# Transposing 8192 x 8192 in fp32: two PSUM counters merged into one, and the load's wait moved onto the first transpose

## The chip, the cores and the metric

One core of a Trainium2 chip. The metric is the device time of one execution in microseconds (us), median of several runs. A difference of under 2% counts as "same".

In the lines of the profile, PE stands for TensorE's matmuls (a transpose is one of them), PEld for its weight loads, DVE for VectorE, ACT for ScalarE; a q behind the name is the engine's sequencer, which waits, branches and issues. `in` is a load buffer, `ps` PSUM, `regs` a store region. L118 is line 118 of that run's kernel, and the numbers shift from kernel to kernel. A semaphore is used in this program as a counter that one side raises (`then_inc`, `sem_inc`) and an engine waits for (`wait_ge`, `wait_op`). A load is said to have landed when its semaphore has the last of the 16 increments that the load's wait asks for.

## The reference

```python
def setup_inputs():
    return {"x": np.random.randn(8192, 8192).astype(np.float32)}

def reference(x):
    return np.transpose(x)
```

268.44 MB have to be read from HBM and 268.44 MB written to it.

## The kernel before

The input is taken in 128 steps. Each step is a chunk of 128 rows x 4096 columns (2 MB), loaded into one of three SBUF buffers. TensorE transposes it in 32 pieces of 128 x 128 into PSUM: 16 pieces fill the first half (`pss[0]`), 16 the second (`pss[1]`). ScalarE copies the first half out into a ring of store regions, VectorE the second half. ScalarE also issues all stores and all loads but the first three, in program order.

TensorE's program is a loop; it waits for the load, then for each half of PSUM:

```python
def transposes(k):
    nc.tensor.sem_inc(s_ld[k], -16).wait_op(s_ld[k], 16, "sem-ge")        # L112
    for q in range(NR):                                                   # NR = 8
        e, g = divmod(q, NH)                                              # NH = 4
        if g == 0:
            nc.tensor.sem_inc(s_bank[e], -1).wait_op(s_bank[e], 1, "sem-ge")   # L116
        for b in range(B):                                                # B = 4
            tr = nc.tensor.transpose(pss[e][...], ins[k][...], ident)     # L118
        if q % 2:
            tr.then_inc(s_pe, 1)
...
for e in range(2):
    nc.tensor.sem_inc(s_bank[e], 1)          # both halves free at the start
nc.tensor.wait_ge(s_id, 2)                   # identity built by GpSimd
```

The copies wait for `s_pe`, and the last of a half gives that half back:

```python
for t, (s, c) in enumerate(chunks):
    for e in range(2):
        eng = (nc.scalar, nc.vector)[e]
        ...                                   # wait for a region's store where a new one begins
        for u in runs:                        # 1 to 4 copies a half
            eng.wait_ge(s_pe, t * NH + (e * NH + u[-1]) // 2 + 1)
            cp = nc.scalar.copy(out=o, in_=i) if e == 0 else nc.vector.tensor_copy(out=o, in_=i)   # L216
            ...
            if u is runs[-1]:
                ...
                cp.then_inc(s_bank[e], 1)     # this half of PSUM is free
            for q in ends:
                store(q, e, copied[e])        # issued by ScalarE
    if t + NIN < T:                           # NIN = 3
        nc.scalar.wait_ge(s_pe, (t + 1) * NR // 2)
        load(t + NIN)                         # into the buffer just transposed
```

Of the kernel before, what the change touches and what calls it, by code (L numbers as in the profile page):

```python
# [39 lines left out]
@with_exitstack  # L40
def kernel(
    ctx: ExitStack,
    tc: tile.TileContext,
    x: bass.AP,
    out: bass.AP,
):








    nc = tc.nc
    P = 128
    N, M = x.shape
    assert x.shape == out.shape[::-1]
    dt = x.dtype

    S = 32
    B = 4
    W = 8
    NR = S // B
    NIN = 3
    NREG = 9
    CH = N // P
    J = S * P

    with tc.tile_critical():  # L70
        nc.alloc_sbuf_tensor("pad", [P, 32], dt)
        ident = nc.alloc_sbuf_tensor("ident", [P, P], dt).ap()
        ins = [nc.alloc_sbuf_tensor(f"in{k}", [P, J], dt).ap() for k in range(NIN)]
        SIZE = B * W * P
        regs = nc.alloc_sbuf_tensor("regs", [P, NREG * SIZE], dt).ap()
        NH = NR // 2
        pss = [nc.alloc_psum_tensor(f"ps{k}", [P, NH * B * P], dt).ap() for k in range(2)]

        s_id = nc.alloc_semaphore("s_id")
        s_ld = [nc.alloc_semaphore(f"s_ld{k}") for k in range(NIN)]  # L80
        s_st = [nc.alloc_semaphore(f"s_st{k}") for k in range(NREG)]
        s_bank = [nc.alloc_semaphore("s_banka"), nc.alloc_semaphore("s_bankv")]
        s_pe = nc.alloc_semaphore("s_pe")
        s_cp = [nc.alloc_semaphore("s_cpa"), nc.alloc_semaphore("s_cpv")]

        nc.gpsimd.memset(ident, 0.0).then_inc(s_id, 1)  # L86
        nc.gpsimd.wait_ge(s_id, 1)
        nc.gpsimd.affine_select(  # L88
            out=ident,
            in_=ident,  # L90
            compare_op=mybir.AluOpType.not_equal,
            fill=1.0,
            base=0,
            pattern=[[-1, P]],
            channel_multiplier=1,
        ).then_inc(s_id, 1)

        chunks = [(s, c) for s in range(M // J) for c in range(CH)]

        def load(t):  # L100
            s, c = chunks[t]
            (nc.sync if t < NIN else nc.scalar).dma_start(
                out=ins[t % NIN], in_=x[c * P:(c + 1) * P, s * J:(s + 1) * J]
            ).then_inc(s_ld[t % NIN], 16)






        def transposes(k):
            nc.tensor.sem_inc(s_ld[k], -16).wait_op(s_ld[k], 16, "sem-ge")  # L112
            for q in range(NR):
                e, g = divmod(q, NH)
                if g == 0:
                    nc.tensor.sem_inc(s_bank[e], -1).wait_op(s_bank[e], 1, "sem-ge")  # L116
                for b in range(B):
                    tr = nc.tensor.transpose(  # L118
                        pss[e][:, (g * B + b) * P:(g * B + b + 1) * P],
                        ins[k][:, q * B * P + b:(q + 1) * B * P - B + b + 1:B],  # L120
                        ident,
                    )
                if q % 2:
                    tr.then_inc(s_pe, 1)



        T = len(chunks)
        assert T % NIN == NIN - 1
        pe = [nc.tensor.engine]  # L130
        for e in range(2):
            nc.tensor.sem_inc(s_bank[e], 1)
        nc.tensor.wait_ge(s_id, 2)
        with nc.Fori(0, T // NIN + 1, engines=pe) as turn:
            with nc.tensor.If(turn > 0):
                transposes(NIN - 1)
            for k in range(NIN - 1):
                transposes(k)

        for t in range(NIN):  # L140
            load(t)

        copied = [0, 0]
        free = list(range(NREG))
        stored = [0] * NREG
        window = {}

        def store(q, e, count):
            t0, r, parts = window.pop(q)
            nc.scalar.wait_ge(s_cp[e], count)  # L150
            base = 0
            for s, a, z in parts:
                rows = (z - a) * P
                j0 = s * J + q * B * P
                dst = out[j0:j0 + B * P, a * P:a * P + rows]
                dst = dst.rearrange("(q b) i -> q b i", q=P)
                src = regs[:, r * SIZE + base:r * SIZE + base + B * rows]
                base += B * rows
                if any(stored):
                    st = wide_dma(nc, nc.scalar, "qActDynamicHW", dst, src)  # L160
                else:
                    st = nc.scalar.dma_start(
                        out=dst, in_=src.rearrange("q (b i) -> q b i", b=B)
                    )
                st.then_inc(s_st[r], 16)
                stored[r] += 1
            free.append(r)

        def closes(w, t):
            t0, r, parts = w  # L170
            return t + 1 == t0 + sum(z - a for _, a, z in parts)
# [5 lines that stand above are left out]
                place = []  # L177
                for q in range(e * NH, (e + 1) * NH):
                    if q not in window:



                        span = (q - c) % W + 1
                        r = free.pop(0)
                        parts = [(s, c, min(c + span, CH))]
                        if c + span > CH and t + span < T:
                            parts.append((s + 1, 0, c + span - CH))
                        window[q] = (t, r, parts)
                        if stored[r]:
                            eng.wait_ge(s_st[r], 16 * stored[r])  # L190
                    t0, r, parts = window[q]
                    k = [p[0] for p in parts].index(s)
                    base = r * SIZE + B * P * sum(z - a for _, a, z in parts[:k])
                    _, a, z = parts[k]
                    place.append((base + (c - a) * P, (z - a) * P))

                runs = []
                for g in range(NH):
                    if runs:
                        u = runs[-1]  # L200
                        gap = place[g][0] - place[g - 1][0]
                        if place[g][1] == place[u[0]][1] and abs(gap) < 2 ** 15 and (
                            len(u) == 1 or gap == place[u[1]][0] - place[u[0]][0]
                        ):
                            u.append(g)
                            continue
                    runs.append([g])
                for u in runs:
                    off, dist = place[u[0]]
                    gap = place[u[-1]][0] - place[u[-2]][0] if len(u) > 1 else 0  # L210
                    dims = [list(regs.ap[0]), [gap, len(u)], [dist, B], [1, P]]
                    o = bass.AP(regs.tensor, regs.offset + off, dims)
                    i = pss[e][:, u[0] * B * P:(u[-1] + 1) * B * P]
                    i = i.rearrange("p (l b i) -> p l b i", b=B, i=P)
                    eng.wait_ge(s_pe, t * NH + (e * NH + u[-1]) // 2 + 1)  # L215
                    cp = nc.scalar.copy(out=o, in_=i) if e == 0 else nc.vector.tensor_copy(out=o, in_=i)  # L216
                    ends = [e * NH + g for g in u if closes(window[e * NH + g], t)]
                    if ends:
                        cp.then_inc(s_cp[e], 1)
                        copied[e] += 1  # L220
                    if u is runs[-1]:
                        if ends:
                            eng.wait_ge(s_cp[e], copied[e])
                            eng.sem_inc(s_bank[e], 1)
                        else:
                            cp.then_inc(s_bank[e], 1)
                    for q in ends:
                        store(q, e, copied[e])
            if t + NIN < T:
                nc.scalar.wait_ge(s_pe, (t + 1) * NR // 2)  # L230
                load(t + NIN)
        for r in range(NREG):
            nc.sync.wait_ge(s_st[r], 16 * stored[r])
# [30 lines left out]
```

## Time and profile before

| | before |
|---|---|
| time, median of 3 runs | 1264.1 us (1263.37 to 1264.13) |
| span of the profiled run | 1262.4 us |
| TensorE busy | 749.6 us, 59% |
| VectorE, ScalarE busy | 24%, 20% |
| DMA | 425 GB/s over the span |
| landing of one load to the next | 9.76 us (median) |

How to read it: here no compute engine is busy over 59%, the DMA digits are 9 in 39 of 40 slices, and the GB/s row lies between 413 and 431 from the second slice to the 39th.

### The profile page before, as it was taken

To read this page: it belongs to the slowest core of one execution; us is meant where nothing else is said; L and a number is where in the kernel's file an instruction comes from. 1 tells how busy PE (TensorE), PEld (TensorE's weight loads), DVE (VectorE), ACT (ScalarE), POOL (GpSimd) and SP (SyncE) were. 2 spreads that over 40 slices of the span, in tenths; PEclk is the share of its full clock that TensorE was granted. 3 is DMA by queue.
4 is the path that set the end of the run, shared out by engine and by line. 5 is a ranking of instruction groups with operands and counts; after the bars stand their busy time and mean duration, and the time that the engine had idled before them with its cause. 6 is when DMAs were issued, how large, how long until landed. Compare 5 with 4: busy or idle time off the path is not lost. (4 is left out here: it accounts for less than half of the span.)

```text
span 1262.4 us, 9794 instructions
## 1 busy us (share of the span) xinstructions
PE 749.6 (59%) x4096; PEld 729.1 (58%) x4096; DVE 302.7 (24%) x250; ACT 252.8 (20%) x257; POOL 0.7 (0%) x6
## 2 busy tenths in 40 slices
PE   6566555656566555656566655666565655666561
PEld 6565555655566555655565655656565655666561
DVE  2322222222222222222222222222222222222220
ACT  3212121121111211122211121121112211121120
POOL 0000000000000000000000000000000000000000
PEclk9967777686767777686866787777768687776865
DMA  9999999999999999999999999999999999999998
GB/s 381 429 429 428 430 430 428 430 429 431 428 430 430 429 428 431 429 429 430 429 423 413 431 428 431 428 430 429 431 428 430 429 430 430 429 430 429 430 419 346
DMA packets 39273, 536.97 MB, mean 425 GB/s; under 512 B 4320, under 2 KB 4832, under 8 KB 6240
## 3 DMA queue, kind: packets, MB, share of 16 engines
q10 hardware_dynamic: 38832, 530.60, 98.8%
q1 hardware_dynamic: 432, 6.29, 1.2%
q14 instruction: 8, 0.07, 0.0%
q8 instruction: 1, 0.02, 0.0%
HBM read 268.44 MB, written 268.44 MB: 425 GB/s over the span
## 5 line engine op out<-in xcount | busy, mean ns | idle before, releaser
L118 PE MATMUL ps<-ident,in 128*128 128x128 f32 x4096 | 749.6, 366 | 486.2 <-PEq L116 486.1
L118 PEld LDWEIGHTS ps<-ident,in 128*128 128x128 f32 x4096 | 729.1, 220 | 506.5 <-issue 506.5
L216 DVE COPY regs<-ps 128x512 f32<-128x512 f32 (+3 forms) x250 | 302.7, 1246 | 934.4 <-PE ps L118 823.4
L216 ACT COPY regs<-ps 128x512 f32<-128x512 f32 (+3 forms) x256 | 251.5, 1015 | 981.9 <-PE ps L118 491.1
L216 ACT ACT_TABLE_LOAD x1 | 1.3, 1283 | 0.9 <-SPq L70 0.9
L88 POOL TENSOR_SCALAR_AFFINE_SELECT ident<-ident 128x128 f32<-128x128 f32 x1 | 0.3, 294 | 0.2 <-POOL ident L86 0.2
L86 POOL MEMSET ident<- 128x128 f32 x1 | 0.2, 205 | 0.5 <-SPq L70 0.5
L248 POOL MEMSET const-bfloat16-1.0<- 128x1 bf16 x1 | 0.1, 102 | 0.0
L248 POOL MEMSET const-uint8-127<- 128x1 uint8 x1 | 0.1, 102 | 0.0
L248 POOL MEMSET const-float32-0.0<- 128x1 f32 x1 | 0.1, 99 | 0.2 <-issue 0.2
L248 POOL MEMSET const-float32-1.0<- 128x1 f32 x1 | 0.1, 99 | 0.0
## 6 DMA issues: line engine op xcount, KB each, us to landing
in<-in_x_dram ACTq DMA_DIRECT2D x125, 2048.0 KB, 21.7
out_dram<-regs ACTq DMA_DIRECT2D x114, 2048.0 KB, 17.5
out_dram<-regs ACTq DMA_DIRECT2D x4, 1792.0 KB, 17.4
in<-in_x_dram SPq DMA_DIRECT2D x3, 2048.0 KB, 11.7
out_dram<-regs ACTq DMA_DIRECT2D x4, 1536.0 KB, 14.8
out_dram<-regs ACTq DMA_DIRECT2D x4, 1280.0 KB, 15.2
out_dram<-regs ACTq DMA_DIRECT2D x4, 1024.0 KB, 15.5
out_dram<-regs ACTq DMA_DIRECT2D x4, 768.0 KB, 16.4
```

The source lines that it names most:

```text
L86: nc.gpsimd.memset(ident, 0.0).then_inc(s_id, 1)
L88: nc.gpsimd.affine_select(out=ident, in_=ident, compare_op=mybir.AluOpType.not_equal, fill=1.0, base=0, pattern=[[-1, P]], channel_multipl ...
L118: tr = nc.tensor.transpose(pss[e][:, (g * B + b) * P:(g * B + b + 1) * P], ins[k][:, q * B * P + b:(q + 1) * B * P - B + b + 1:B], ident,)
L216: cp = nc.scalar.copy(out=o, in_=i) if e == 0 else nc.vector.tensor_copy(out=o, in_=i)
L248: nc = _bacc.Bacc("TRN2", target_bir_lowering=False, num_devices=1)
```

## The change

The intent is to have fewer instructions on TensorE's sequencer: one wait for PSUM a step, not two; the load's wait carried by the first transpose; and no start-up increments, since GpSimd sets PSUM free when the identity is built. As written, TensorE has nine semaphore instructions fewer: two in each of the three steps of its loop's body, and three before the loop.

```diff
-        s_bank = [nc.alloc_semaphore("s_banka"), nc.alloc_semaphore("s_bankv")]
+        s_bank = nc.alloc_semaphore("s_bank")
...
         nc.gpsimd.affine_select(...)
-        ).then_inc(s_id, 1)
+        ).then_inc(s_bank, 2)
...
         def transposes(k):
-            nc.tensor.sem_inc(s_ld[k], -16).wait_op(s_ld[k], 16, "sem-ge")
+            nc.tensor.sem_inc(s_bank, -2).wait_op(s_bank, 2, "sem-ge")
             for q in range(NR):
                 e, g = divmod(q, NH)
-                if g == 0:
-                    nc.tensor.sem_inc(s_bank[e], -1).wait_op(s_bank[e], 1, "sem-ge")
                 for b in range(B):
                     tr = nc.tensor.transpose(...)
+                    if q == b == 0:
+                        tr.wait_op(s_ld[k], 16, "sem-ge").then_inc(s_ld[k], -16)
...
-        for e in range(2):
-            nc.tensor.sem_inc(s_bank[e], 1)
-        nc.tensor.wait_ge(s_id, 2)
...
-                            cp.then_inc(s_bank[e], 1)
+                            cp.then_inc(s_bank, 1)
```

There is a second effect beside the count. With one counter that must reach 2, TensorE cannot start the first half of a step before VectorE has copied the second half of the step ahead.

More of the change, by code (lines that the diff above doesn't have):

```diff
@@ L223 @@
                             eng.wait_ge(s_cp[e], copied[e])
-                            eng.sem_inc(s_bank[e], 1)
+                            eng.sem_inc(s_bank, 1)
                         else:
-                            cp.then_inc(s_bank[e], 1)
+                            cp.then_inc(s_bank, 1)
                     for q in ends:
```

## The prediction

> **What bounds the kernel now.** I read the page first (busy shares, slices, DMA queues), then the waits, then the timeline at the start, in the middle and at the end, then the same stretches as a table of windows.
>
> The page:
>
> ```profile
> PE 749.6 (59%) x4096; PEld 729.1 (58%) x4096; DVE 302.7 (24%) x250; ACT 252.8 (20%) x257; POOL 0.7 (0%) x6
> DMA  9999999999999999999999999999999999999998
> GB/s 381 429 429 428 430 430 428 430 429 431 428 430 430 429 428 431 429 429 430 429 423 413 431 428 431 428 430 429 431 428 430 429 430 430 429 430 429 430 419 346
> q10 hardware_dynamic: 38832, 530.60, 98.8%
> in<-in_x_dram ACTq DMA_DIRECT2D x125, 2048.0 KB, 21.7
> ```
>
> No engine is busy over 59% of the span, while the DMA engines are at nine tenths or more in every slice but the last, and move 428 to 431 GB/s from the second slice to nearly the end. The bytes are fixed: 268.44 MB in, 268.44 MB out. 536.9 MB at 429 GB/s is 1251.5 us; the span is 1262.4. So at most 11 us of the whole program are anything but transfers at the rate that they show. The last line gives the depth of the queue: a load lands 21.7 us after its issue, and a step (one 128x4096 chunk) takes 9.76 us (median distance of two loads' landings), so about two steps of work stand in the queue all the time.
>
> Where is the DMA not full? The windows (length; busy us of PE, PEld, DVE, ACT, POOL; clock; DMA share; GB/s):
>
> ```profile
> 0.00:2.00 2.00, 0.00 (x0) 0.00 (x0) 0.00 (x0) 1.10 (x1) 0.70 (x6) 1.00 0.19 41
> 2.00:1227.00 1225.00, 742.94 (x4064) 722.60 (x4064) 299.91 (x246) 249.32 (x253) 0.00 (x0) 0.75 1.01 428
> 1227.00:1229.00 2.00, 0.00 (x0) 0.00 (x0) 0.31 (x1) 0.00 (x0) 0.00 (x0) 0.83 0.64 270
> 1229.00:1256.00 27.00, 6.65 (x32) 6.49 (x32) 2.50 (x4) 2.35 (x4) 0.00 (x0) 0.56 1.00 419
> 1256.00:1263.00 7.00, 0.00 (x0) 0.00 (x0) 0.00 (x0) 0.00 (x0) 0.00 (x0) 0.50 0.13 56
> ```
>
> For 1225 us the share is 1.01. Idle are the first 2 us, some 0.7 us at 1227 to 1229, and the run-out after 1256.
>
> The waits say what TensorE waits for:
>
> ```profile
> PE ps L118 <- PEq L116: 486.1, 126, 8.6
> ACT regs L216 <- DMA out_dram<-regs: 478.8, 61, 10.2
> ```
>
> The 486 us look like a wait for PSUM (L116), the very wait that the change merges. That is a trap: L116 is only the last of the sequencer's instructions before the matmul. In the trace's records the wait for the load (L112) starts 0.03 us after the load's sixteenth completion, the first L116 some 0.15 us later, and the first weight load 0.26 us after the landing, in nearly every step. So TensorE waits for data.
>
> [...] two L116 instructions stand 0.17 us apart although each shows 0.05 us. [...] Here all stores and all loads but three are issued by ScalarE in program order, which the change does not touch: only a gap in the queue could change the time, not an order.
>
> **The change, part by part.**
>
> 1. One counter in place of two. Before, TensorE may write the first half of PSUM as soon as ScalarE has copied it, and the second half as soon as VectorE has. Now a step starts when both have copied. What counts is the room between the last copy's end of step t and the landing of load t+1. The steady state looks like this (start, length, engine):
>
> ```profile
> 1042.97 5.56 PE L118 MATMUL ps<-ident,in 128*128 128x128 f32 x32 [4.19 <-PEq L116]
> 1047.65 1.87 ACT L216 COPY regs<-ps 128x2048 f32<-128x2048 f32 x1 [7.84 <-DMA out_dram<-regs]
> 1048.57 2.29 DVE L216 COPY regs<-ps 128x2048 f32<-128x2048 f32 x1 [7.46 <-PE ps L118]
> 1052.74 6.16 PE L118 MATMUL ps<-ident,in 128*128 128x128 f32 x32 [4.21 <-PEq L116]
> ```
>
> The last copy ends at 1048.57 + 2.29 = 1050.86, TensorE starts again at 1052.74 because the load landed at 1052.45: 1.6 us of room. I listed this for all 127 step changes from the trace's records. From step 5 on the room is never negative: median 1.59 us, least 0.38 us (after step 55). Put the other way, matmuls 5.6 us (6.7 at worst, under a lowered clock) plus 1.9 us (2.6 at worst) until the last copy's end make 7.5 us, 9.4 at worst, in a step of 9.76 us. So the merged wait should cost TensorE nothing there.
>
> At the start it does bind. The three first loads land at 8.28, 13.10 and 18.13, closer than a step:
>
> ```profile
> 8.56 14.10 PE L118 MATMUL ps<-ident,in 128*128 128x128 f32 x96 [8.56 <-PEq L116]
> 13.67 2.48 DVE L216 COPY regs<-ps 128x512 f32<-128x512 f32 x4 [13.67 <-PE ps L118]
> 17.54 2.48 DVE L216 COPY regs<-ps 128x512 f32<-128x512 f32 x4 [1.39 <-PE ps L118]
> 21.73 2.48 DVE L216 COPY regs<-ps 128x512 f32<-128x512 f32 x4 [1.71 <-PE ps L118]
> ```
>
> VectorE's copies of step 0 end at 16.15, but step 1 began at 14.31. It will now begin at about 16.2 and end its matmuls at about 20.3 (4.1 us at full clock). VectorE ends 1.55 us after that, at 21.9, so step 2 runs from 22.0 to 26.1 (before: 18.5 to 22.7), step 3 from about 27.8 (before 25.3), step 4 from 33.5 to 35 (before 31.4), and by step 7 (load at 53.4) the plan is caught up. TensorE is up to 3.5 us late. Does the DMA queue run dry from it? Load 4 is issued when step 1's matmuls are done: 20.3 instead of 18.5. Counting bytes issued less bytes moved in the trace of before, 2.4 MB stood in the queue just ahead of its issue at 18.5, so about 1.85 MB at 20.3. Load 5 moves from 22.7 to 26.2: before, 4.28 MB stood at 27, which without that load (2.1 MB) and the store that may also come late (0.8 MB) leaves 1.4 MB, 3 us of transfers. Later steps have more. So the queue never runs dry: cost 0.
>
> 2. The wait for the load moves onto the first transpose, two semaphore instructions a step are gone. 256 of them in 128 steps, with the three before the loop some 259 fewer executed. Copies that wait on a store's landing by themselves start 0.02 us after it; I estimate landing to first weight load at 0.05 to 0.15 us instead of 0.26. That is 0.1 to 0.2 us earlier a step, 13 to 26 us over 128 steps if TensorE were the bound. It is not: a load issued 0.2 us earlier only stands 0.2 us longer in the queue. It shows in the time at one place, the dip at 1227, where the queue waits for the store that follows step 126's copies: up to 0.2 us.
>
> 3. GpSimd's release instead of two increments by TensorE: done at about 1.7 us, the first load lands at 8.28. Cost 0.
>
> Sum: 0 (steady) + 0 (start) - 0.1 (end) us on 1264.1.
>
> **The rivals.** (a) The merged wait makes TensorE and the copies one serial loop and this becomes the bound. For it: the smallest room is 0.38 us, and the clock of TensorE is uneven. Against it: 7.5 us against 9.76 us, and a late step only eats of a queue two steps deep. If it held at every step by 0.3 us, 128 x 0.3 = 38 us, 1302. (b) The late start drains the queue: at most TensorE's 3.5 us, 1267.6. The 1.4 MB left speak against it. (c) The saved instructions shorten the path: 26 us at most, 1238, if TensorE set the pace; the DMA row speaks against it.
>
> **Range and chances.** The median should be 1264.0 us. The three runs of before span 0.8 us; rival (b) in part would add 1 to 3 us[...]. So 1262.0 to 1266.5 holds it 8 times in 10. Two per cent is 25 us: faster 0.01, same 0.98, slower 0.01.
>
> **What would show it.** TensorE's wait should now be put down to the load (in<-in_x_dram), not to its sequencer; landing to first weight load about 0.1 us; step 1's matmuls after 16.1; step 2's end near 26; the DMA row unchanged, its second slice at 429 GB/s still; instructions near 9,536 of 9,794. A second slice below 425 GB/s would prove rival (b); a gap between copies and landing gone in mid-run with a DMA digit below 9, rival (a). I am wrong if the DMA's rate itself depends on when TensorE starts, which nothing here shows.

0 + 0 - 0.1 us on 1264.1 us makes the 1264.0 us predicted. The 0.05 to 0.15 us from landing to first weight load stand as the estimate, from the 0.02 us in which copies followed a store's landing.

## The result

| | before | changed |
|---|---|---|
| median | 1264.05 us (6 runs, 1263.37 to 1264.13) | 1263.94 us (6 runs, 1263.13 to 1264.64) |
| ratio | | 1.000 (95% interval 0.9987 to 1.0013) |

A ratio here and below is the mean time of one kernel's fast runs over the mean of the other's fast runs of the same rounds, so it is not quite the ratio of the medians.

The page of the changed kernel has the same rows as before:

```profile
PE 746.5 (59%) x4096; PEld 725.9 (58%) x4096; DVE 302.8 (24%) x250; ACT 252.9 (20%) x257; POOL 0.7 (0%) x6
DMA  9999999999999999999999999999999999999998
GB/s 387 427 430 428 428 431 427 430 430 430 429 429 431 428 430 430 429 429 431 426 426 416 429 428 431 430 428 430 430 429 430 430 429 430 431 430 428 431 425 346
```

Its waits tell who ended TensorE's idle time (us in total, times, longest):

```profile
PE ps L116 <- DMA in<-in_x_dram: 472.2, 120, 8.3
PE ps L116 <- PEq L112: 15.9, 8, 2.8
```

What was 486 us "until L116" is now 472 us until the load, with the same idle time in sum. The new name is the true one: before, the semaphore instruction for PSUM (L116), which started 0.156 us after the load's (L112) in the median of 128 steps, stood between it and the matmul and took the blame. The 8 waits of 15.9 us are the real waits for PSUM, and they all lie at the start. TensorE's timeline shows them (start, length, idle time before it and what ended it):

```profile
15.81 4.11 PE L116 MATMUL ps<-ident,in 128*128 128x128 f32 x32 [1.85 <-PEq L112]
21.77 5.57 PE L116 MATMUL ps<-ident,in 128*128 128x128 f32 x32 [1.85 <-PEq L112]
29.20 4.08 PE L116 MATMUL ps<-ident,in 128*128 128x128 f32 x32 [1.85 <-PEq L112]
...
64.40 4.11 PE L116 MATMUL ps<-ident,in 128*128 128x128 f32 x32 [2.82 <-PEq L112]
72.26 5.56 PE L116 MATMUL ps<-ident,in 128*128 128x128 f32 x32 [3.75 <-DMA in<-in_x_dram]
```

Between the matmuls of one step and the next 1.85 to 1.93 us pass in the first seven of these, and 2.82 us in the eighth: VectorE's copies and the hand-over (in the first, 1.54 us until the copies end at 15.50 and 0.31 us more to the matmul). From step 9 (72.26) on the load ends the wait, as here in mid-run, where the last copy ends at 1047.66 + 2.29 = 1049.95, 1.86 us before the next step's matmuls:

```profile
1047.66 2.29 DVE L213 COPY regs<-ps 128x2048 f32<-128x2048 f32 x1 [7.49 <-PE ps L116]
1051.81 6.09 PE L116 MATMUL ps<-ident,in 128*128 128x128 f32 x32 [4.19 <-DMA in<-in_x_dram]
```

First weight loads of the steps, in us, from the two traces' records:

| step | 1 | 2 | 3 | 4 | 5 | 6 | 7 | 8 | 9 |
|---|---|---|---|---|---|---|---|---|---|
| before | 14.31 | 18.52 | 25.29 | 31.38 | 38.12 | 45.48 | 53.69 | 62.98 | 72.65 |
| changed | 15.78 | 21.74 | 29.16 | 35.11 | 42.52 | 50.02 | 55.99 | 64.37 | 72.23 |

TensorE is up to 4.5 us late, and the transfers do not notice. The windows of both kernels over that stretch and over the rest, first the kernel before, then the changed one (the last two columns are DMA share and GB/s):

```profile
15.00:64.00 49.00, 32.04 (x229) 30.91 (x229) 18.43 (x27) 14.45 (x19) 0.00 (x0) 0.93 1.01 419
64.00:1225.00 1161.00, 703.63 (x3797) 684.59 (x3797) 278.15 (x215) 232.53 (x229) 0.00 (x0) 0.74 1.01 429
```

```profile
15.00:64.00 49.00, 34.56 (x224) 33.43 (x224) 17.66 (x26) 14.59 (x19) 0.00 (x0) 0.86 1.01 420
64.00:1225.00 1161.00, 699.64 (x3808) 680.43 (x3808) 279.53 (x218) 232.53 (x229) 0.00 (x0) 0.74 1.01 429
```

419 and 420 GB/s, 429 and 429. Bytes issued less bytes moved, between 18 and 60 us, never fall below 2.6 MB before and 1.5 MB after (a packet counted as moved when it ends): the late loads ate 1 MB of a queue that held enough.

### The profile page after: what moved, and what is told of

Its sections match the earlier page's. It is cut to its first block, busy times and chain, and to the rows that moved or that the text cites. A ratio compares the mean times of both kernels' runs of the same rounds, so it can differ in the third digit from the quotient of the medians.

```text
span 1261.3 us, 9664 instructions
## 1 busy us (share of the span) xinstructions
PE 746.5 (59%) x4096; PEld 725.9 (58%) x4096; DVE 302.8 (24%) x250; ACT 252.9 (20%) x257; POOL 0.7 (0%) x6
## 4 chain that ended last, share of the span: by engine, by line
DMA 75%; PE 10%; DVE 4%; ACT 3%; ACTq 1%; issue 1%; DVEq 0%
DMA in<-in_x_dram 42%; DMA out_dram<-regs 33%; PE ps L116 10%; DVE regs L213 4%; ACT regs L213 3%; ACTq L28 1%; DVEq L212 0%; ACTq L221 0%
## 5 line engine op out<-in xcount | busy, mean ns | idle before, releaser
L116 PE MATMUL ps<-ident,in 128*128 128x128 f32 x4096 | 746.5, 365 | 488.1 <-DMA in<-in_x_dram 472.2
L116 PEld LDWEIGHTS ps<-ident,in 128*128 128x128 f32 x4096 | 725.9, 220 | 508.6 <-issue 508.6
```

The lines of the kernel that those rows point to most:

```text
L116: tr = nc.tensor.transpose(pss[e][:, (g * B + b) * P:(g * B + b + 1) * P], ins[k][:, q * B * P + b:(q + 1) * B * P - B + b + 1:B], ident,)
```

## The experiments

Kernels that are compared with each other below ran on the same chip, in rounds with the plain kernel before; the ratios are to that kernel's runs of the same rounds.

### The two parts alone

`p1_one_counter`: the changed kernel with the load's wait back in an instruction of its own.

```diff
         def transposes(k):
+            nc.tensor.sem_inc(s_ld[k], -16).wait_op(s_ld[k], 16, "sem-ge")
             nc.tensor.sem_inc(s_bank, -2).wait_op(s_bank, 2, "sem-ge")
...
-                    if q == b == 0:
-                        tr.wait_op(s_ld[k], 16, "sem-ge").then_inc(s_ld[k], -16)
```

> One part alone: the two PSUM counters are merged, the load keeps its own semaphore instruction ahead of the PSUM wait. Theory (transfers set the pace, a queue of over 1.5 MB always stands in front of them): 1264.0 us, within 1 us of before; steps 1 to 8 start late by 1 to 5 us as in the changed kernel, landing to first weight load back at about 0.26 us from step 9 on. Rival (the serial loop of matmuls and copies costs something that the shorter landing-to-start of the changed kernel pays back): 1264 + 0.15 x 128 = 1283 us.

Measured: 1263.54 us, ratio to before 0.9997 (0.9983 to 1.0011). Landing to first weight load: 0.26 us in the median; five late steps at the start, not eight.

`p2_wait_on_transpose`: the kernel before with the load's wait on the first transpose.

```diff
         def transposes(k):
-            nc.tensor.sem_inc(s_ld[k], -16).wait_op(s_ld[k], 16, "sem-ge")
...
+                    if q == b == 0:
+                        tr.wait_op(s_ld[k], 16, "sem-ge").then_inc(s_ld[k], -16)
```

> The other part alone: two PSUM counters as before, the wait for the load on the first transpose. Theory: 1264.0 us, within 1 us of before, with landing to first weight load shorter than 0.26 us (0.10 to 0.2) and no late start beyond that of before. Rival (landing to start is on the path): 0.1 to 0.16 us x 128 = 13 to 20 us less, 1244 to 1251 us.

Measured: 1263.84 us, ratio 0.9996 (0.9982 to 1.0009). Landing to first weight load fell to 0.10 us in this kernel too. So the result is not a gain and a loss that cancel: each part alone is worth nothing here, and a start that is 0.15 us earlier in each of 128 steps did not save the 20 us that the rival made of it.

### Is the serial loop there at all? More work for VectorE

Each VectorE copy is made two or three times (each waits for the one ahead of it; the results stay right). The same edit in both kernels:

```diff
+                    for _ in range((1 or 2) if e else 0):
+                        nc.vector.tensor_copy(out=o, in_=i).then_inc(s_x, 1)
+                        extra += 1
+                        nc.vector.wait_ge(s_x, extra)
                     cp = nc.scalar.copy(...) if e == 0 else nc.vector.tensor_copy(...)
```

Twice, in the kernel before and in the changed one:

> Kernel before, every VectorE copy made twice, results right. Second half of the matmuls 2.8 us + 2.4 + 2.3 us of copies + 0.3 = 7.8 us against 9.76 us. Theory: 1264 to 1272 us (the last step's copies take 2.4 us longer).

> Changed kernel, every VectorE copy made twice, results right: the second threshold test. Loop: 5.6 us of matmuls at the granted clock of the full-transfer kernel + 1.86 us + one more copy of 2.45 us + 0.27 us = 10.2 us against 9.76 us. Theory: 128 x 10.2 + 15 = 1320 us, 1270 to 1350, above the kernel before with two copies by 1 to 6%.

Measured: 1266.43 us with two counters (ratio to the plain kernel 1.002, 0.9996 to 1.0048) and 1343.48 us with one (1.063, 1.061 to 1.065). The same extra copies are hidden with two counters and cost 6% with one (1.0628 / 1.0022 = 1.060). The timeline of the second kernel, TensorE and then VectorE in the middle of the run, shows the loop:

```profile
603.12 6.64 PE L117 MATMUL ps<-ident,in 128*128 128x128 f32 x32 [5.22 <-PEq L113]
614.98 5.93 PE L117 MATMUL ps<-ident,in 128*128 128x128 f32 x32 [5.21 <-PEq L113]
```

```profile
609.80 1.76 DVE L215 COPY regs<-ps 128x1536 f32<-128x1536 f32 x1 [6.98 <-PE ps L117]
611.60 1.76 DVE L218 COPY regs<-ps 128x1536 f32<-128x1536 f32 x1
613.27 0.68 DVE L215 COPY regs<-ps 128x512 f32<-128x512 f32 x1
613.99 0.69 DVE L218 COPY regs<-ps 128x512 f32<-128x512 f32 x1
```

The matmuls end, four copies follow one after the other, the last ends at 614.68, and only then the next matmuls start, 0.30 us later. The load is not what ends this wait. A step took 10.26 us in the median (estimate: 10.2), more than the 9.76 us of its transfers. The mean granted clock was 0.798, against 0.744 in the changed kernel, although TensorE was busy for less of the time (53% against 59%); why was not tested.

The DMA digits would not have told that the transfers no longer set the pace here; the GB/s row does (400 GB/s in the mean, where the real kernels have 425 and 426):

```profile
DMA  8789999999999999999999999999999999999998
GB/s 337 281 328 416 405 415 401 412 426 395 416 391 423 425 413 410 425 374 395 398 397 426 386 425 400 420 396 415 410 409 423 395 417 393 422 430 409 405 401 344
```

Three times:

> Kernel before, every VectorE copy made three times (each waits for the one ahead of it), results right. VectorE's share of a step grows from 2.4 to about 7.2 us. With two counters only the second half of the matmuls waits for it: 2.8 us of matmuls + 6.9 us of copies + 0.3 = 10.0 us at worst against a step of 9.76 us. Theory: 1264 to 1300 us.

> Changed kernel, every VectorE copy made three times, results right. With one counter all matmuls of a step wait for it: 4.9 to 5.6 us of matmuls + 1.9 us + two more copies of 2.4 us + 0.27 us = 11.9 to 12.6 us a step. Theory (the merged counter does make a serial loop, which the room of 1.6 us hides in the real kernel): 128 x 12.2 = 1560 us, 1500 to 1630, over 15% slower than the same copies with two counters. Rival (the merged counter makes no serial loop, the matmuls of a half still go ahead): within 2% of the kernel before with three copies.

Measured: 1337.48 us with two counters (1.056) and 1722.82 us with one (1.363); one to the other 1.290. The direction is as expected, both sizes are over the range. With one counter a step took 13.22 us where 11.9 to 12.6 were expected; its matmuls took 6.11 us in the median, not 4.9 to 5.6, at a mean granted clock of 0.668. With two counters a step took 10.16 us in the median against "10.0 at worst", over the 9.76 us of the plain kernel, and the DMA row fell to 7 in the second and third slices, so the transfers no longer set the pace there either. Its waits show ScalarE idle for 387.5 us until "issue"; ScalarE issues the stores of VectorE's half and waits for those copies in its own program order, which the estimate had left out. How much of the 37 us over the range is due to that was not separated.

### Is the transfer what hides it? Fewer bytes stored

Only one of the four output rows that each partition holds is stored ("light"), or two of them ("half"). The output is wrong, all other work is the same:

```diff
+                dst, src = dst[:, :1], src[:, :rows]          # light;  half: dst[:, :2], src[:, :2 * rows]
                 if any(stored):
                     st = wide_dma(nc, nc.scalar, "qActDynamicHW", dst, src)
```

Light, in four kernels:

> Kernel before with a quarter of each store (one of the four rows that each partition holds), so the output is wrong on purpose. A step then moves 2.10 + 0.52 = 2.62 MB, 6.1 us at 429 GB/s, against 9.76 us. Theory (transfers set the pace, TensorE and copies have 5 to 6 us of work a step in two overlapped halves): 128 x 6.1 + 12 = 793 us, 780 to 830.

> Changed kernel with the same quarter stores, output wrong on purpose. Theory: the loop of matmuls, last copy and hand-over is now longer than the transfers; in the changed kernel's own first steps, where data were there, this loop took 6.9 us (15.8 to 64.4 in seven steps). 128 x 6.9 + 14 = 900 us, 860 to 980: 8 to 20% slower than the kernel before with the same stores. Rival (the merged counter costs nothing in any regime, since TensorE catches up at a higher clock): within 2% of it.

> Merged counter alone with quarter stores. Theory: the same loop as in the changed kernel; if the load's own semaphore instruction runs ahead of the PSUM wait it adds nothing, if it stands in the loop it adds up to 0.15 us a step, 19 us. So the changed kernel's light time, up to 19 us more.

> Wait for the load on the transpose alone, two counters, quarter stores. Theory: as the kernel before with quarter stores within 1%, since transfers set the pace there too. Rival (landing to start is on the path once the queue is shorter): up to 20 us less.

| light stores | median, us | ratio to the plain kernel | step, us (median) |
|---|---|---|---|
| kernel before | 816.32 | 0.647 (0.643 to 0.651) | 6.12 |
| changed | 897.13 | 0.710 (0.707 to 0.713) | 6.74 |
| one counter alone | 869.79 | 0.688 (0.685 to 0.690) | 6.59 |
| wait on the transpose alone | 811.14 | 0.630 (0.627 to 0.634) | 6.13 |

With lighter transfers the changed kernel is slower than the kernel before by 0.7098 / 0.647 = 1.097, as expected (8 to 20%). The last row is uncertain: three of its five runs (811 to 827 us) are marked slow in the record, the ratio comes from the other two (795 and 800 us), and the profiled run is a slow one. Those two fast runs lie some 20 us under the kernel before with light stores (0.6304 / 0.647 = 0.974), as the rival had it, not within the 1% of the theory; the slow ones lie where that kernel's runs do (814 to 825 us). So whether the shorter landing to start saves time with light stores stays open; it does no harm.

One thing went against the expectation: the changed kernel was to be the faster of the two with one counter, and is the slower by 0.7098 / 0.6875 = 1.032, 27 us. The timelines tell why. Changed kernel, light, TensorE and VectorE:

```profile
405.32 4.11 PE L116 MATMUL ps<-ident,in 128*128 128x128 f32 x32 [2.76 <-PEq L112]
412.12 4.08 PE L116 MATMUL ps<-ident,in 128*128 128x128 f32 x32 [2.70 <-PEq L112]
```

```profile
409.47 2.35 DVE L214 COPY regs<-ps 128x1536 f32<-128x1536 f32 x2 [4.45 <-PE ps L116]
```

One counter alone, light:

```profile
402.44 4.11 PE L117 MATMUL ps<-ident,in 128*128 128x128 f32 x32 [2.54 <-PEq L113]
```

```profile
399.93 2.35 DVE L213 COPY regs<-ps 128x1536 f32<-128x1536 f32 x2 [4.26 <-PE ps L117]
```

VectorE ends at 409.47 + 2.35 = 411.82 and the next matmul starts at 412.12: 0.30 us. In the other kernel it is 402.28 and 402.44: 0.16 us. Over all steps the median from the last copy's end to the first weight load is 0.272 us and 0.116 us. In the changed kernel the wait for PSUM comes first in the program and the wait for the load behind it; when PSUM is what comes last, as in these two runs, the second instruction still has to be gone through: 0.272 - 0.116 = 0.156 us. 0.156 x 127 = 20 us of the 27 us follow from that; the other 7 us are not accounted for. So of the loss of 9.7% the one counter by itself makes 0.6875 / 0.647 = 6.3%; the rest is mostly the order of the two waits.

A kernel with the two swapped, PSUM's wait and decrement on the transpose, was not run.

Half stores, a test of the threshold, with a transfer step of 7.33 us (estimate, 3.15 MB at the 429 GB/s of the kernel before) just above the loop (6.74 us with light stores):

> Kernel before with half of each store, output wrong on purpose. A step moves 2.10 + 1.05 = 3.15 MB, 7.33 us at 429 GB/s. Theory: 128 x 7.33 + 12 = 950 us, 940 to 975.

> Changed kernel with half of each store, output wrong on purpose: a threshold test. Its loop took 6.7 to 6.9 us a step when quarter stores let it run free, so a transfer step of 7.33 us should just hide it, with room of some 0.4 us. Theory: within 2% of the kernel before with half stores, 945 to 985 us. Rival (the merged counter costs 0.6 us a step whenever TensorE is not idle most of the time): 128 x 0.6 = 77 us more, 1027 us.

Measured: 951.18 us and 965.19 us, ratio of the two 0.7651 / 0.7525 = 1.017. The waits of the changed kernel stand on the edge, 59 times for the load and 69 times for PSUM:

```profile
PE ps L116 <- DMA in<-in_x_dram: 173.3, 59, 8.4
PE ps L116 <- PEq L112: 165.8, 69, 2.9
```

The steps' first weight loads tell where the difference arises: of 7.9 us by the last step (profiled runs) 7.5 us were there at step 9, and the 60 later waits for PSUM added 0.4 us.

So the cost goes from 9.7% to 1.7% (which counts as "same") to nothing as a step's transfers go from 6.1 to 7.3 to 9.8 us, with a loop of about 6.7 us. In these three pairs of kernels that is a threshold: the cost is gone where the transfers of a step last longer than the loop by enough (9.8 against 6.7 us); a cost for each step would have stayed.

## Why the prediction was right

Time: 1264.0 predicted, 1263.94 measured. That they agree to 0.1 us is luck, as the six runs of each kernel span 0.8 and 1.5 us; that nothing changed is not luck. By its steps:

1. "The merged wait should cost TensorE nothing there" (steady state): right. From step 9 on every wait of TensorE is for the load, and the doubled copies and the light stores show that the loop exists and that room hides it. Its "7.5 us, 9.4 at worst" adds medians and worst cases of different steps (and 6.7 + 2.6 is 9.3): from the first matmul to the last copy a step of the kernel before took 7.9 us in the median, 9.1 at worst. The room that it listed by step, 1.59 and 0.38 us, is right.
2. "The queue never runs dry" (start): right. Ahead of load 5, for which 1.4 MB were estimated, 1.9 MB stood. But "Later steps have more" was wrong, the least is 1.5 MB at 48.6 us; and 1.85 MB at 20.3 does not follow from "2.4 MB" (2.4 - 1.8 us x 0.429 = 1.6), only from the 2.6 MB counted as above. The estimate of the lateness was too small: 4.5 us, not 3.5, and caught up at step 9, not 7. Two terms were mis-sized. The hand-over was taken as 0.1 us and is 0.27 us from copy to weight load (seven of the eight late steps). And 4.1 us of matmuls, at full clock (4.11 us at a granted clock of 1.00 at 31.41 in the kernel before), were taken for step 1 and for step 2; four of the eight late steps (2, 4, 5, 7) took 5.56 or 5.57 us.
3. "0.05 to 0.15 us instead of 0.26" (landing to first weight load): right, 0.104 us. Its reason, that the transpose would wait by itself as the copies do, was wrong. In the changed kernel's trace the wait is a semaphore instruction again, at the transpose's own line (128 of them), and nothing stands between it and the weight load: 0.104 us where it was 0.260. The pair that it cited, two L116 instructions 0.17 us apart, has the 16 transposes of a half between them; the pair with nothing between is L112 and the next L116, 0.156 us from start to start where each shows 0.051. The views of the single lines show it, first before (L112 load, L116 PSUM), then changed (L112 PSUM, L116 load):

```profile
L112 PEldq EVENT_SEMAPHORE  x128: 51/51/51, 8.3 to 1228.9; - x128
L116 PEldq EVENT_SEMAPHORE  x256: 51/51/51, 8.5 to 1229.2; - x128
```

```profile
L112 PEldq EVENT_SEMAPHORE  x128: 51/51/51, 1.7 to 1226.2; - x128
L116 PEldq EVENT_SEMAPHORE  x128: 51/51/51, 8.2 to 1227.9; - x128
```

Of 384 such instructions 256 are left. The prediction had 256 of them gone and "instructions near 9,536"; the page has 9,664. Only the decrement rides on the matmul: in the changed kernel's trace the records of the 128 first matmuls carry it, and the semaphore instructions at L116 carry the wait alone.

4. "Up to 0.2 us" at the dip near 1227: the DMA share there went from 0.64 to 0.93 in the profiled runs, but the time moved by 0.1 us, within the spread of the runs. Not shown.
5. The rivals: (a) is a real mechanism, shown with the doubled and tripled copies and the light stores, and lay 1.6 us of room away; (b) and (c) did not occur.
6. "What would show it": TensorE's waits and the landing came as said. Step 1's matmuls started at 15.81, not after 16.1, since VectorE's copies of step 0 ended at 15.50 already, not at 16.15; step 2 ended at 27.3, not near 26; the second slice had 427 GB/s, not 429. The sign for rival (a), a DMA digit below 9, was too blunt: with doubled copies and one counter the loop set the pace under digits of 9.

## What to carry to other kernels

Before merging two waits into one, measure the room: from the last thing that will now be waited for to the moment at which the data arrive. Here 1.6 us of room hid a loss of overlap that, with the order of the waits, costs 9.7% when three quarters of each store are left out, and an instruction count would have shown neither. When two waits stand one behind the other, ask which is satisfied last: with light stores the kernel that had that one in the last place was the faster by 27 us (869.79 against 897.13). And do not read the name in a wait's line as its cause when several waits stand in a row: here 486 us stood under the wait for PSUM and were for the load.
